# A decoder trunk step on one core: dense products inside the norm sums, the state copied by ScalarE, the next pair's first part beside the inverse, and steps that wait for a PSUM bank

## The chip, the cores and the metric

The kernel runs on one core of a Trainium2 chip. The time is device microseconds of one execution, the median of a few runs. The core has five engines that run their own instruction streams and wait for one another through semaphores: TensorE (PE in the profile, its weight loads PEld), VectorE (DVE), ScalarE (ACT), GpSimd (POOL) and SyncE (SP, which here only issues transfers).

## The reference, cut to what matters

One layer of a recurrent decoder trunk for 1024 prompt tokens and 8 sequences of 8 sample tokens (1088 columns, NT), width 1024, eight heads of 64. The recurrence of a head, whose matrix state is S:

```
def step(S, inp):
    r_t, w_t, k_t, v_t, kk_t, a_t = inp
    sa = einsum("bhvk,bhk->bhv", S, -kk_t)
    S = S * w_t + sa[..., None] * (kk_t * a_t) + v_t[..., None] * k_t
    y = einsum("bhvk,bhk->bhv", S, r_t)
    return S, y

h = adaLN(RMSNorm(x), c);  P = h @ w_in
r, k, v, xw, xa, xg = split(token_shift(P))
w_logit = w0 + tanh(xw) @ w2;  a = sigmoid(a0 + xa @ a2)
kk = k * k_k;  kk = kk * rsqrt(sum(kk * kk, per head) + 1e-12)
y = group_norm(scan(step)) + bonus;  o_r = y * (sigmoid(xg) @ g2)
merged = g_r * (o_r @ w_br_rwkv) + g_p * (o_p @ w_br_pool)
x = x + gate * (merged @ w_out)
x = x + gate2 * (relu(adaLN(RMSNorm(x), c) @ w_ff1) ** 2 @ w_ff2)
```

`o_p` comes from a pooling branch (running means over 2, 4, 8 and 16 tokens, then a small product per group).

## The kernel before

**Dense products.** An fp32 product is made of three products of rounded halves (`mm3`: high·high, high·low, low·high). A weight tile is split by ScalarE (`whi`, L193) and by VectorE or GpSimd (`wlo`, L194). A dense step is one 128x128 weight block on one of three column chunks (364, 362, 362): three TensorE products into an `mm` bank of PSUM. A job is a block of output rows: 72 such products with `w_in`. When a job is done, ScalarE mostly empties its banks (`px`, L531, L564, L582), and the next job opens three others. PSUM has eight banks: four `mm`, two `w` for the recurrence's steps, two `wc` for the state.

**First phase.** 34 jobs with `w_in`, then eight with `w_br` (`op_job`), run as a *back* stream. Between its steps runs *fore* work, generators that yield a time or a condition: `chains` (index 0), `heads` (1), `pools` (2), `or_rows` (3). TensorE's order is fixed by hand: `Pace.run` keeps a model clock `t`, which each product moves on by a modelled duration. A generator whose time has come takes the next turn, otherwise the back stream does. `Pace.warm` holds a step back until the last 3.4 us of the model hold enough dense work. The other engines' order is made by the framework from the order in which the program issues instructions.

**The recurrence** handles four pairs of heads, f = 0 to 3, in chunks of 64 tokens (two units u of eight chunks for the prompt, a third for the sample tokens):

- `front(f)`: squares of `kk`, `rinv` (the norm: nine products of a 128x128 block with the two columns `hsel`, two instructions each in TensorE's trace; root; reciprocal; spread over 64 columns on ScalarE), `spread` (128x128 transposes, `w<-kct,wt`), decay and gate logits (`w<-wt,sw`) with Tanh, then the cumulated decays `ev`, the scaled keys `bk` and the last decay of each chunk, `end`.
- `scores`: products of `ra` and `bk` for each unit, the bonus, transposes.
- `inverse` (a chain on VectorE), `level` (four steps of 32x32 products) and `affine`: `first` makes z·w and z·uv (`w<-at,z`, `w<-uv,z`), `second` (`w<-ab,at`) makes the transition matrix of each chunk in `ra[:, :, 1]`.
- `chain(f)`: sixteen state steps. Each is two products into `pn` (`wc<-ra,S`), the new S = S·end + pn on VectorE (L994), and two into `py`. Steps stand 2300 apart in the model's clock (1500 for the last pair).
- `sample(f)` and `post(f)`: the sample tokens' state, group norm (again `rinv` and `spread`) and gate. `post(3)` writes its result into the rows that the first job of phase 2 reads.

`heads` runs, for each f: `front(f)` and `scores(f)` side by side with `sample(f-1)`; then inverse, level and affine side by side with `post(f-1)`. `both` merges two generators: all of their steps that are due run within one turn of `Pace.run`. So `front(f+1)`, which needs nothing of the state, runs beside `chain(f)`.

**Second phase** (merge, output product, MLP, final norm) follows; its order is the same in both kernels.

Of the kernel before, what the change touches and what calls it, by code (L numbers as in the profile page):

```python
# [9 lines left out]
F32 = mybir.dt.float32  # L10
# [3 lines left out]
ALU = mybir.AluOpType  # L14
# [4 lines left out]
P = 128  # L19
# [60 lines left out]
class Pace:  # L80
# [3 lines left out]
    def __init__(self):  # L84
        self.t = 0.0
        self.work = []
        self.dense = False

# [15 lines left out]

    def run(self, back, fore=(), until=lambda: False):
        live = {i: 0.0 for i in range(len(fore))}
# [30 lines left out]
class K:  # L137
# [64 lines left out]
    def ps(self, tag):  # L202
        return (self.pc if tag == "wc" else self.pp).tile([P, 512], F32, tag=tag, bufs=PB[tag], name=self.nm(tag))
# [143 lines left out]
    def rinv(self, x, blocks, scale, eps, R):  # L347

        nc, k = self.nc, len(blocks)
        ps = self.ps("w")  # L350
        for i, b in enumerate(blocks):
            self.mm(ps[:, 2 * i:2 * i + 2], x[:, b:b + 128], self.kc("hsel"), start=True, stop=True)
        r = self.cp.tile([P, 9, 2], F32, tag="rh", bufs=3, name=self.nm("rh"))[:, :k, :]
        f = r.rearrange("p k h -> p (k h)")
        nc.scalar.activation(f, ps[:, :2 * k], AF.Sqrt, bias=self.eps[:, eps:eps + 1], scale=scale)
        nc.vector.reciprocal(f, f)
        i = 0
        for x in R:
            m = x.shape[1] // 128
            nc.scalar.activation(x.rearrange("p (k h j) -> p k h j", h=2, j=64), r[:, i:i + m, :].unsqueeze(3).to_broadcast([P, m, 2, 64]), AF.Copy)  # L360
            i += m
        return [x[:, o:o + 128] for x in R for o in range(0, x.shape[1], 128)]
# [286 lines left out]
    def front(self, f):  # L649
# [15 lines left out]
        yield self.pace.warm(8000 if f else 11000)  # L665
# [8 lines left out]
        for c0, n in FP:  # L674
            ps = self.ps("w")
            self.mm(ps[:, :n], w2a2[0:64, :], wa[0:64, c0:c0 + n], start=True, stop=True)
            nc.scalar.activation(t1[:, c0:c0 + n], ps[:, :n], AF.Tanh, bias=self.hp[:, f:f + 1], scale=0.5)
# [6 lines left out]
        nc.sync.dma_start(r, self.d_x[f])  # L684
        e = self.row(self.p1, "e", 1, w=1112)
# [6 lines left out]
        if f:  # L692
            yield lambda: ("c", f - 1, 0) in self.done
        for c0, n in FH:
            s, cs = slice(c0, c0 + n), slice(c0 // 64, (c0 + n) // 64)
            t, a, x = t1[:, s], tha[:, s], k[:, s]
            nc.vector.tensor_scalar(t, t, 1.0, None, op0=ALU.add)
            nc.vector.tensor_tensor_scan(t, self.kscan[:, s], t, 0.0, ALU.mult, ALU.add)  # L698
            m = min(n, NPR - c0)
# [9 lines left out]
            for h, hs in enumerate(HB):  # L709
                nc.vector.tensor_tensor(bk[hs, cs, h, :], cut(x[hs]), cut(t[hs]), op=ALU.mult)  # L710
                nc.vector.scalar_tensor_tensor(bk[hs, cs, 1 - h, :], cut(a[hs]), 0.5, cut(t[hs]), op0=ALU.mult, op1=ALU.mult)  # L711
            if c0 == 0:
                self.cur = dict(bk=bk, end=end, kk=kk, r=r, ev=ev, es=es, z=self.z, qs={})
                self.ra(self.cur, 0)
        nc.gpsimd.tensor_copy(end[:, 0:16], ev[:, :, 64])
        nc.gpsimd.tensor_copy(end[:, 16:24], es[:, :, 8])
# [5 lines left out]
        self.cur.update(q=q, v=v)  # L722

# [34 lines left out]
    def unit(self, f, d, u):  # L758
# [21 lines left out]
        yield 9000 if u == 0 else 3000 if u == 1 else 2000  # L780
# [150 lines left out]
    def affine(self, f, d):  # L931
# [4 lines left out]
        def first(u):  # L936
# [8 lines left out]
            nc.vector.tensor_copy(uv[HB[1], :, 0, :], cut(pu[HB[1], :]))  # L945
            nc.scalar.activation(uv[HB[0], :, 1, :], cut(pu[HB[0], :]), AF.Copy)

        def second(u):
            Q = d["qs"][u]
            ab, ra, w = Q["ab"], Q["ra"], Q["at"]  # L950
            pss = [self.ps("w") for _ in range(2)]
# [5 lines left out]
            for a, ps in enumerate(pss):  # L957
                pv = ps.rearrange("p (c s j) -> p c s j", s=2, j=64)
                us = slice(4 * a, 4 * a + 4)
                nc.scalar.activation(ra[:, us, 1, :], pv[:, :, 1, :], AF.Copy)  # L960
# [9 lines left out]
    def chain(self, f, d):  # L970

        nc = self.nc
        end = d["end"]
        S = None
        for u in range(2):
# [9 lines left out]
            for i in range(8):  # L985
                c = 8 * u + i
                at = slice(i * 64, (i + 1) * 64)
                S1 = self.sm.tile([P, 64], F32, tag="S", bufs=3, name=self.nm("S"))
                if S is None:
                    nc.vector.tensor_copy(S1, pn[:, at])  # L990
                else:
                    for hs in HB:
                        self.mm(pn[hs, at], ra[hs, i, 1, :], S[hs, :], start=False, stop=True, skip_group_check=True)
                    nc.vector.scalar_tensor_tensor(S1, S, end[:, c:c + 1], pn[:, at], op0=ALU.mult, op1=ALU.add)  # L994
# [148 lines left out]
    def heads(self):  # L1143

        for f in range(4):
            def lead():
                yield from self.front(f)
                yield from self.scores(f, self.cur)
# [8 lines left out]
            fill = self.post(f - 1) if f else self.ada_fill()  # L1157
            self.ds[f] = d

# [5 lines left out]
            yield from self.both(main(), fill)  # L1165
# [3 lines left out]
    def ada_fill(self):  # L1169
        wt = lambda: self.wt()[:, :1024]  # L1170
        asb = self.wt()[:, :512]
        yield from self.ada_part("w_ada_mix", 2, wt, asb, self.am, "b_mix", (16, 20), 5000)

# [17 lines left out]
    def chains(self):  # L1191
        for f in range(4):
# [53 lines left out]
    def phase1(self, ctx):  # L1246
# [38 lines left out]
        self.orr = [[None] * 4 for _ in range(2)]  # L1285
        self.pace.run(back, [self.chains(), self.heads(), self.pools(), self.or_rows()])
        nc.scalar.dma_start(io["o_ns"], self.ns)
# [764 lines left out]
```

## Time and profile before

| | us |
|---|---|
| median of three runs | 1656.93 |
| lowest and highest | 1653.72 and 1657.07 |
| the profiled execution, its own time | 1654.8 |
| its span in the trace | 1653.0 |
| TensorE busy in it | 1597.1 |
| VectorE, ScalarE, GpSimd busy | 1040.3, 721.7, 364.6 |

Rows of the profile name engine, line, operation and tiles as output<-inputs; `w<-ACT wt L677` among the waits says that a TensorE instruction that writes a `w` tile waited for ScalarE's instruction of line 677. The granted clock is the share of TensorE's full clock in a stretch (1.00 or 0.50 here). Line numbers are those of the kernel before; the kernel after has the dense product's line at 184 instead of 170 and the transpose's at 191 instead of 177.

### The profile page before, as it was taken

What the parts mean: (1) busy time and instruction counts of PE and PEld (TensorE: products, weight loads), DVE (VectorE), ACT (ScalarE), POOL (GpSimd) and SP (SyncE); (2) the same over time, 40 slices, a digit from 0 to 9 for tenths busy, and PEclk for the clock granted to TensorE, in tenths of its full rate; (3) what the DMA queues carried; (4) which work ended last, traced back from release to release, by engine and by line L of the source; (5) the groups of instructions that cost most, each with busy time, mean ns of one, the idle gap of its engine ahead of it and who ended that gap; (6) DMA issues with size and microseconds to landing.
All of it is one profiled execution on the core that took longest, in us unless ns stands there. A gap on an engine that the chain in (4) does not pass through costs nothing.

```text
span 1653.0 us, 35432 instructions
## 1 busy us (share of the span) xinstructions
PE 1597.1 (97%) x14331; PEld 1488.8 (90%) x14331; DVE 1040.3 (63%) x1800; ACT 721.7 (44%) x1414; POOL 364.6 (22%) x459
## 2 busy tenths in 40 slices
PE   6999999999999999999999999999999999999997
PEld 3989878887888889979989999999999999999997
DVE  5686547744675466334553696777555677877866
ACT  5543333343334333412233475545444765553323
POOL 3320101100000000001631332323233342521231
PEclk9999999999999999999999999999999999999999
DMA  9333413331332242375976455666665965675313
GB/s 338 111 110 135 139 48 119 117 102 67 113 109 92 80 136 102 103 295 174 348 251 227 131 181 180 220 226 240 232 222 204 347 202 190 195 247 182 99 39 109
DMA packets 123333, 279.43 MB, mean 169 GB/s; under 512 B 16769, under 2 KB 31105, under 8 KB 123169
## 3 DMA queue, kind: packets, MB, share of 16 engines
q1 hardware_dynamic: 107808, 228.52, 40.4%
q0 software_dynamic: 9312, 32.41, 5.9%
q10 hardware_dynamic: 6048, 16.23, 2.8%
q8 instruction: 113, 1.85, 0.5%
q14 instruction: 52, 0.42, 0.1%
HBM read 198.15 MB, written 78.95 MB: 168 GB/s over the span
## 4 chain that ended last, share of the span: by engine, by line
PE 82%; DVE 7%; ACT 4%; DMA 3%; issue 3%; POOL 1%; SPq 0%; DVEq 0%; ACTq 0%; POOLq 0%
PE mm L170 36%; PE pr L170 30%; PE w L170 11%; PE wc L170 4%; DMA wraw<-in_w_out 1%; PE w L177 1%; DVE hx L1729 1%; DMA x<-in_xT 1%; ACT whi L193 1%; DVE wlo L194 1%; DVE bk L711 0%; DVE wt L698 0%; POOL wlo L194 0%; DVE bk L710 0%; DMA wr<-in_w_ff 0%
## 5 line engine op out<-in xcount | busy, mean ns | idle before, releaser
L170 PE MATMUL mm<-hx,whi 128*128 128x362 f32 (+1 forms) x1920 | 507.8, 346 | 6.8 <-ACT px L564 2.9
L170 PEld LDWEIGHTS mm<-hx,whi 128*128 128x128 f32 x1920 | 334.0, 190 | 43.2 <-issue 18.5
L170 PE MATMUL pr<-mr,whi 128*128 128x272 f32 x1792 | 336.5, 287 | 0.6 <-DVE hx L1729 0.6
L170 PE MATMUL mm<-hx,wlo 128*128 128x362 f32 (+1 forms) x960 | 316.1, 329 | 0.0
L170 PEld LDWEIGHTS pr<-mr,whi 128*128 128x128 f32 x1792 | 280.7, 188 | 2.8 <-issue 2.8
L170 PE MATMUL pr<-mr,wlo 128*128 128x272 f32 x896 | 257.9, 288 | 0.2 <-DVE wlo L194 0.2
L193 ACT ACTIVATE whi<-wraw 128x512 fp32r<-128x512 f32 x186 | 116.9, 630 | 232.3 <-PE mm L170 68.9
L194 DVE TENSOR_TENSOR wlo<-wraw,whi 128x512 fp32r<-128x512 f32 x145 | 112.1, 773 | 121.1 <-ACT whi L193 120.9
L170 PEld LDWEIGHTS mm<-hx,wlo 128*128 128x128 f32 x960 | 182.9, 190 | 0.0
L170 PE MATMUL pr<-hx,whi 128*128 128x272 f32 x896 | 168.7, 287 | 1.4 <-DVE rs L1924 0.8
L170 PEld LDWEIGHTS pr<-mr,wlo 128*128 128x128 f32 x896 | 168.6, 188 | 0.4 <-DVE wlo L194 0.4
L170 PE MATMUL mm<-mr,whi 128*128 128x272 f32 (+4 forms) x736 | 152.3, 301 | 0.0
L170 PEld LDWEIGHTS pr<-hx,whi 128*128 128x128 f32 x896 | 140.3, 188 | 2.6 <-ACT whi L193 1.0
L193 ACT ACTIVATE whi<-wr 128x512 fp32r<-128x512 f32 x138 | 86.4, 628 | 112.6 <-PE pr L170 80.4
L170 PE MATMUL pr<-hx,wlo 128*128 128x272 f32 x448 | 128.9, 288 | 0.0
L170 PEld LDWEIGHTS mm<-mr,whi 128*128 128x128 f32 x736 | 119.2, 188 | 3.0 <-issue 2.5
L170 PE MATMUL mm<-mr,wlo 128*128 128x272 f32 (+4 forms) x368 | 110.2, 299 | 0.0
L194 POOL TENSOR_TENSOR wlo<-wraw,whi 128x512 fp32r<-128x512 f32 x41 | 55.3, 1349 | 245.8 <-ACT whi L193 245.6
L194 DVE TENSOR_TENSOR wlo<-wr,whi 128x512 fp32r<-128x512 f32 x103 | 77.2, 752 | 17.4 <-ACT whi L193 17.3
L170 PE MATMUL pr<-t,whi 128*128 128x272 f32 x448 | 84.6, 287 | 0.0
L170 PEld LDWEIGHTS pr<-hx,wlo 128*128 128x128 f32 x448 | 84.3, 188 | 0.0
L170 PEld LDWEIGHTS pr<-t,whi 128*128 128x128 f32 x448 | 70.2, 188 | 0.8 <-issue 0.8
(398 smaller groups left out, 2704.9 us busy)
## 6 DMA issues: line engine op xcount, KB each, us to landing
wr<-in_w_ff SPq DMA_DIRECT2D x137, 256.0 KB, 3.4
hid<-d_ch POOLq DMA_DIRECT2D x72, 272.0 KB, 3.7
wraw<-in_w_ff SPq DMA_DIRECT2D x71, 256.0 KB, 3.1
wraw<-in_w_in SPq DMA_DIRECT2D x68, 256.0 KB, 3.0
d_ch<-hx SPq DMA_DIRECT2D x52, 272.0 KB, 3.7
hid<-in_w_ada_mlp SPq DMA_DIRECT2D x24, 512.0 KB, 6.6
d_th<-px SPq DMA_DIRECT2D x22, 544.0 KB, 2.9
wt<-d_x SPq DMA_DIRECT2D x20, 544.0 KB, 4.3
```

What stands on the lines that cost most here:

```text
L170: return self.nc.tensor.matmul(out, lhsT, rhs, **kw)
L177: self.nc.tensor.transpose(out, in_, ident)
L193: nc.scalar.activation(hi, raw, AF.Copy)
L194: (nc.gpsimd if pool else nc.vector).tensor_tensor(lo, raw, hi.bitcast(F32), op=ALU.subtract)
L1729: nc.vector.tensor_tensor(acc, acc, v, op=ALU.add)
```

## The change

Four edits.

1. **Norm sums.** After every two products with `hsel`, `rinv` calls `pace.fill()`, which takes one dense step from the back stream. At its end ScalarE does a Tanh on one column, which loads Tanh's table again at that place.
2. **State.** `second` adds the diagonal matrix of the chunk's `end` to the transition matrix (GpSimd makes it, VectorE adds it while it empties the bank; before, ScalarE copied). The state step then is products and one ScalarE copy. The copies of `uv` and `end` go to ScalarE, too.
3. **Order of a pair.** `front` is cut in two. The first part, up to the Tanhs, runs for pair f + 1 beside inverse, level and affine of pair f, behind `post(f-1)`. The rest is `burst`, which gives way between its operations for f > 0 and stands beside `chain(f-1)`. Its wait for the state of the first unit moves to its end, ahead of `ra`. Some gaps change (Tanh steps 1300 to 2000; `warm` 8000 to 12000; the first unit's 9000 to 3000 for f > 0), and the first chain waits for the `w_ada_mix` part.
4. **Banks.** `Pace` models the two `w` banks. A step of `heads`, or a timed step of `pools`, is held back while both are taken. A step that opens banks takes them for 1500 to 3000 of the model's clock.

```diff
+    def fill(self):
+        if next(self.back, "idle") != "idle":
+            self.dense = True
     def run(self, back, fore=(), until=lambda: False):
...
                 r = live[i]
+                if self.taken is not None and i and self.banks[0] > self.t and (i == 1 or i == 2 and not callable(r) and self.t < r + 2500):
+                    continue
                 if r() if callable(r) else r <= self.t:
+                    if self.taken is not None:
+                        self.taken = 0
                     try:
                         r = next(fore[i])
+                        if self.taken:
+                            n = min(self.taken, 2)
+                            self.banks = sorted(self.banks[n:] + n * [self.t + (1500 if callable(r) else min(max(r, 1500), 3000))])
...
         for i, b in enumerate(blocks):
+            if i and i % 2 == 0:
+                self.pace.fill()
             self.mm(ps[:, 2 * i:2 * i + 2], x[:, b:b + 128], self.kc("hsel"), start=True, stop=True)
...
+        nc.scalar.activation(last, R[-1][:, 0:1], AF.Tanh)
...
-        yield self.pace.warm(8000 if f else 11000)
+        yield self.pace.warm(12000 if f else 11000)
...
-            yield 1300
+            yield 2000
...
-        if f:
-            yield lambda: ("c", f - 1, 0) in self.done
...
-        nc.gpsimd.tensor_copy(end[:, 0:16], ev[:, :, 64])
-        nc.gpsimd.tensor_copy(end[:, 16:24], es[:, :, 8])
+        nc.scalar.activation(end[:, 0:16], ev[:, :, 64], AF.Copy)
+        nc.scalar.activation(end[:, 16:24], es[:, :, 8], AF.Copy)
...
+        if f:
+            yield lambda: ("c", f - 1, 0) in self.done
+            self.ra(self.cur, 0)
...
-        yield 9000 if u == 0 else 3000 if u == 1 else 2000
+        yield (3000 if f else 9000) if u == 0 else 3000 if u == 1 else 2000
...
-            nc.vector.tensor_copy(uv[HB[1], :, 0, :], cut(pu[HB[1], :]))
+            nc.scalar.activation(uv[HB[1], :, 0, :], cut(pu[HB[1], :]), AF.Copy)
...
+            dg = cut(self.hv())
+            for hs in HB:
+                nc.gpsimd.tensor_tensor(dg[hs], self.kc("ident")[hs, hs].unsqueeze(1).to_broadcast([64, 8, 64]),
+                                        d["end"][hs, 8 * u:8 * u + 8].unsqueeze(2).to_broadcast([64, 8, 64]), op=ALU.mult)
...
-                nc.scalar.activation(ra[:, us, 1, :], pv[:, :, 1, :], AF.Copy)
+                nc.vector.tensor_tensor(ra[:, us, 1, :], pv[:, :, 1, :], dg[:, us, :], op=ALU.add)
...
-                    nc.vector.scalar_tensor_tensor(S1, S, end[:, c:c + 1], pn[:, at], op0=ALU.mult, op1=ALU.add)
+                nc.scalar.activation(S1, pn[:, at], AF.Copy)
...
-            fill = self.post(f - 1) if f else self.ada_fill()
+            def fill():
+                yield from self.post(f - 1) if f else self.ada_fill()
+                if f < 3:
+                    yield from self.front(f + 1)
```

How this moves TensorE's instructions, at three places. In these rows a name is output<-inputs, then the shape of the moving operand.

The norm sum of pair 1's front on TensorE before: nine products with `hsel` in one run, between a state step and dense products.

```order
L170 MATMUL wc_2496<-ra_1132,S_2720 64x64 x2
L170 MATMUL w_2753<-kct,wt_2667 128x2 x9
L170 MATMUL mm_2650<-hx_354,whi_2625 128x362
L170 MATMUL mm_2650<-hx_355,whi_2625 128x362
L170 MATMUL mm_2650<-hx_354,wlo_2626 128x362
```

The same norm sum in the changed kernel (its first three pieces), now earlier, behind the second affine step of pair 0.

```order
L184 MATMUL w_2483<-ab_1203,at_1206 64x128 x8
L184 MATMUL w_2504<-kct,wt_2320 128x2 x2
L184 MATMUL mm_2353<-hx_356,whi_2333 128x364
L184 MATMUL mm_2353<-hx_357,whi_2333 128x364
L184 MATMUL mm_2353<-hx_356,wlo_2334 128x364
L184 MATMUL w_2504<-kct,wt_2320 128x2 x2
L184 MATMUL mm_2354<-hx_356,whi_2333 128x362
L184 MATMUL mm_2354<-hx_357,whi_2333 128x362
L184 MATMUL mm_2354<-hx_356,wlo_2334 128x362
L184 MATMUL w_2504<-kct,wt_2320 128x2 x2
```

The run of nine has become pieces of two with three dense products between.

The logits of pair 1 (`w<-wt,sw`) on TensorE before, with a state product of the sample tokens (`x,z`) and the opening of a chain unit (`wc<-uv,ab`, `wc<-ab,uv`) behind them.

```order
L170 MATMUL w_2829<-wt_2671,sw_2664 128x512
L170 MATMUL w_2832<-wt_2671,sw_2664 128x512
L170 MATMUL w_2835<-x_2677,z 64x64 x2
L170 MATMUL wc_2840<-uv_1630,ab_1628 64x64 x16
L170 MATMUL wc_2841<-ab_1628,uv_1630 64x64 x16
L170 MATMUL wc_2840<-S_2781,ra_1625 64x64 x2
L170 MATMUL wc_2841<-ra_1625,S_2781 64x64 x2
L170 MATMUL w_2880<-wt_2671,sw_2664 128x288
L170 MATMUL w_2883<-wt_2671,sw_2664 128x288
```

In the changed kernel: the affine steps of pair 0's second unit, the opening of its chain (`wc`), and pair 1's transposes (L191); then, some rows on, the same logits.

```order
L184 MATMUL w_2546<-uv_1665,z 64x64
L191 MATMUL w_2582<-kct,wt_2320 128x128 x4
L184 MATMUL wc_2588<-uv_1205,ab_1203 64x64 x16
L184 MATMUL wc_2589<-ab_1203,uv_1205 64x64 x16
L184 MATMUL w_2627<-ab_1663,at_1666 64x128 x8
L184 MATMUL w_2628<-ab_1663,at_1666 64x128 x8
L191 MATMUL w_2649<-kct,wt_2320 128x128 x4
```

```order
L184 MATMUL w_2705<-wt_2324,sw_2317 128x512
L184 MATMUL w_2708<-wt_2324,sw_2317 128x512
L184 MATMUL wc_2588<-S_2655,ra_1179 64x64 x2
L184 MATMUL wc_2589<-ra_1179,S_2655 64x64 x2
L184 MATMUL mm_2690<-hx_348,whi_2466 128x364
L184 MATMUL mm_2690<-hx_349,whi_2466 128x364
L184 MATMUL mm_2690<-hx_348,wlo_2467 128x364
```

Six more dense products follow these before the next logits, so nine products stand between two uses of the `w` banks; in the affine string before them, transposes of one generator stand directly between the products of the other, with no dense product from the first affine product of this unit to the state step behind the last transpose.

The end of the recurrence on TensorE before: the last transposes (`w_8604`, `w_8610`) and the first rows behind them, which belong to jobs with `w_br`.

```order
L170 MATMUL mm_8557<-hx_8134,wlo_8489 128x364
L170 MATMUL mm_8558<-hx_8134,whi_8488 128x362
L170 MATMUL mm_8558<-hx_8136,whi_8488 128x362
L170 MATMUL mm_8558<-hx_8134,wlo_8489 128x362
L177 MATMUL w_8604<-kct,wt_8320 128x128 x4
L177 MATMUL w_8610<-kct,sw_8318 128x128
L170 MATMUL mm_8559<-hx_8134,whi_8488 128x362
```

The same place in the changed kernel; `mm_8801` is the first bank of phase 2's first job.

```order
L184 MATMUL mm_8687<-hx_8003,whi_8622 128x362
L184 MATMUL mm_8687<-hx_8005,whi_8622 128x362
L184 MATMUL mm_8687<-hx_8003,wlo_8623 128x362
L191 MATMUL w_8740<-kct,wt_8450 128x128 x4
L191 MATMUL w_8746<-kct,sw_8448 128x128
L184 MATMUL mm_8801<-hx_8007,whi_8775 128x364
```

Before, two whole jobs and three products (75) follow the last transposes inside the first phase; now none.

More of the change, by code (lines that the diff above doesn't have):

```diff
@@ L87, in __init__ @@
         self.dense = False
+        self.taken, self.banks = None, [0.0, 0.0]
     def spend(self, t, share):
@@ L202, in ps @@
     def ps(self, tag):
+        if tag == "w" and self.pace.taken is not None:
+            self.pace.taken += 1
         return (self.pc if tag == "wc" else self.pp).tile([P, 512], F32, tag=tag, bufs=PB[tag], name=self.nm(tag))
@@ L684, in front, with burst @@
         nc.sync.dma_start(r, self.d_x[f])
+        self.cur = dict(k=k, kk=kk, t1=t1, tha=tha, r=r)
+    def burst(self, f):
+        nc, io = self.nc, self.io
+        X = lambda b: lambda: ("X", b) in self.done
+        k, kk, t1, tha, r = (self.cur[x] for x in ("k", "kk", "t1", "tha", "r"))
+        step = lambda t: t if f else 0
         e = self.row(self.p1, "e", 1, w=1112)
@@ L698, in front @@
             nc.vector.tensor_tensor_scan(t, self.kscan[:, s], t, 0.0, ALU.mult, ALU.add)
+            yield step(1800)
             m = min(n, NPR - c0)
@@ L1143, in heads @@
     def heads(self):
+        yield from self.front(0)
         for f in range(4):
             def lead():
-                yield from self.front(f)
+                yield from self.burst(f)
                 yield from self.scores(f, self.cur)
@@ L1163, in main @@
                 yield from self.affine(f, d)
-            yield from self.both(main(), fill)
+            yield from self.both(main(), fill())
         yield from self.sample(3, d)
```

20 lines of the change are left out of this document (13 added, 7 removed).

## The prediction

> **What bounds the kernel now.** I read the page first, then the table by stage, then TensorE's waits, then its clock, then its timeline.
>
> ```profile
> PE 1597.1 (97%) x14331; PEld 1488.8 (90%) x14331; DVE 1040.3 (63%) x1800; ACT 721.7 (44%) x1414; POOL 364.6 (22%) x459
> 0.00:50.00 50.00, 34.94 (x177) 20.30 (x178) 31.98 (x57) 25.35 (x37) 18.23 (x39) 0.97 0.89 296
> 50.00:850.00 800.00, 774.70 (x8043) 694.14 (x8042) 460.27 (x856) 297.41 (x634) 102.35 (x158) 0.99 0.39 135
> 850.00:1653.00 803.00, 787.47 (x6116) 774.39 (x6114) 548.05 (x888) 398.93 (x744) 244.05 (x263) 1.00 0.57 195
> ```
>
> The columns of the last three rows are: stretch, length, busy time (and instructions) of PE, PEld, DVE, ACT, POOL, then the granted clock, DMA share and GB/s. TensorE is the bound, 97% busy. The change touches only the stage from about 50 to 850 us, where the recurrence runs between dense products; start and second phase keep their order. In that stage TensorE is idle for 800.00 − 774.70 = 25.3 us. The change neither adds nor removes a product, so it can gain only those 25.3 us, and what a lowered clock costs. TensorE's waits in the stage, longest first (engine, destination, line, what ended the wait; total us, times, longest):
>
> ```profile
> PE w L170 <- ACT wt L677: 5.7, 8, 2.0
> PE wc L170 <- DVE S L994: 4.3, 4, 2.8
> PE mm L170 <- ACT px L564: 2.9, 3, 1.8
> PE w L170 <- DVE wt L1115: 1.9, 2, 1.0
> PE mm L170 <- ACT px L582: 1.5, 1, 1.5
> PE w L170 <- issue: 1.3, 1, 1.3
> PE mm L170 <- DVE px L1319: 1.2, 1, 1.2
> PE w L170 <- DVE px L642: 1.2, 3, 0.6
> ...
> PE w L177 <- ACT z L928: 0.7, 1, 0.7
> PE w L177 <- ACT wt L360: 0.7, 1, 0.7
> PE w L170 <- ACT at L944: 0.7, 1, 0.7
> ```
>
> The rows into `w` add to 5.7 + 1.9 + 1.2 + 0.7 + 0.7 + 0.7 = 10.9 us (1.3 more has no releaser): a head step opens one of two `w` banks before ScalarE or VectorE has emptied it. The rows into `mm` (2.9 + 1.5 + 1.2 = 5.6 us) are dense products waiting for an evacuation. 4.3 us are waits for the state S.
>
> The granted clock is 0.99, not 1. Stretches around the places where it falls (same columns):
>
> ```profile
> 230.37:233.78 3.41, 3.41 (x33) 3.22 (x32) 2.46 (x6) 1.90 (x4) 0.00 (x0) 1.00 0.10 32
> 233.79:237.20 3.41, 3.41 (x19) 2.89 (x18) 0.28 (x1) 1.63 (x4) 0.00 (x0) 0.50 0.12 43
> 421.52:424.93 3.41, 0.65 (x4) 0.34 (x3) 3.35 (x8) 0.00 (x0) 0.03 (x1) 1.00 0.22 72
> 424.94:428.34 3.40, 3.38 (x17) 3.26 (x18) 2.02 (x3) 0.47 (x1) 0.00 (x0) 0.50 0.72 211
> 561.47:564.87 3.40, 3.40 (x15) 3.40 (x15) 0.27 (x1) 1.62 (x4) 0.00 (x0) 0.50 0.00 0
> 564.88:568.29 3.41, 3.41 (x18) 2.81 (x18) 0.28 (x1) 0.38 (x1) 0.00 (x0) 0.50 0.03 10
> ```
>
> There are six such half-clock stretches in the stage: these four, and 401.04 to 404.45 and 517.10 to 520.50. Two follow idle time (421.52: busy 0.65 of 3.41 us, waiting for S). Four follow or contain a norm sum, with TensorE 'busy' throughout: 18 products of two columns each. TensorE's timeline there:
>
> ```profile
> 229.91 0.49 PE L170 MATMUL mm<-hx,whi 128*128 128x364 f32 x2
> 230.24 0.33 PE L170 MATMUL mm<-hx,wlo 128*128 128x364 f32 x1
> 230.50 0.33 PE L170 MATMUL wc<-S,ra 64*64 64x64 f32 x4
> ...
> 230.88 2.17 PE L170 MATMUL w<-kct,wt 128*128 128x2 f32 x18
> ...
> 234.14 0.81 PE L170 MATMUL mm<-hx,whi 128*128 128x364 f32 x2
> 234.75 0.50 PE L170 MATMUL mm<-hx,wlo 128*128 128x364 f32 x1
> ...
> 244.78 0.33 PE L170 MATMUL w<-x,z 64*64 64x64 f32 x4 [2.05 <-ACT wt L677]
> ```
>
> Two dense products start 0.33 us apart at 229.91, 0.165 each; at 234.14 0.61, 0.305 each. A half-clock stretch of dense products thus loses 3.41 × (1 − 0.165 / 0.305) = 1.6 us, six at most 9.4; since small products beside them lose less I count 8.
>
> **The change part by part.** *Norm sums.* The 18 narrow products took 2.17 us, about 0.11 each, and keep that; between every two now stands one dense step of three products (0.5 us). Same work, other order; a split costs between nothing and the longer first dense product (at 229.91 a pair takes 0.49; behind such a run I see up to 0.09 more), so 31 splits cost 0 to 2.8 us. I take 1, with the few further changes of tile shape. In return any 3.4 us then hold more dense work than narrow: I expect three of the four stretches behind norm sums to go, and one of the two behind idle time, since its wait goes: 4 × 1.35 = −5.5 us (bounds 0 and −8).
>
> [...]
>
> *Bank waits.* The model of the pace now holds a head step back while both `w` banks are taken, and tanh steps wait 2000 instead of 1300. The 2.05 us at 244.78 is such a place: two 512-wide and two state products stood directly behind one another; now nine dense products (1.5 us) stand between. But steps merged side by side (inverse and the next front) run back to back without that check: the four SPREAD products now stand directly behind the 32 of the first affine step, whose banks are emptied by ScalarE copies of 0.6 us. I added up, for each reuse of a bank in the new order, the products that cover it, at the durations above: about 9 us remain of 12.2 (10.9 + 1.3). I take −3; bounds −10 and +3.
>
> *State.* Rows that carry this (line, engine, operation, shapes, count | busy us, mean ns | idle before):
>
> ```profile
> L994 DVE SCALAR_TENSOR_TENSOR S<-S,end,wc 128x64 f32<-128x64 f32 x60 | 16.7, 278 | 31.4 <-PE wc L170 25.6 <-PE w L170 5.1
> L533 ACT ACTIVATE px<-mm 128x64 f32<-128x64 f32 x13 | 3.0, 228 | 0.0
> L960 ACT ACTIVATE ra<-w 128x256 f32<-128x256 f32 x16 | 5.9, 380 | 10.8 <-PE w L170 10.8
> L961 DVE TENSOR_TENSOR ra<-ra,w 128x256 f32<-128x256 f32 x16 | 6.6, 420 | 15.0 <-ACT ra L960 14.7
> L946 ACT ACTIVATE uv<-w 64x512 f32<-64x512 f32 x8 | 4.7, 591 | 3.1 <-DVE uv L945 3.1
> L355 ACT ACT_TABLE_LOAD x8 | 10.3, 1283 | 0.1
> L194 POOL TENSOR_TENSOR wlo<-wraw,whi 128x512 fp32r<-128x512 f32 x14 | 18.6, 1326 | 144.7 <-ACT whi L193 144.7
> ```
>
> 60 state updates of 278 ns leave VectorE; 64 copies of about 228 ns come to ScalarE. The 16 copies of L960 (380) become 16 additions of 420 on VectorE; eight uv copies (0.59) move to ScalarE; the table loads rise by 4 net (1.28). ScalarE: 64 × 0.228 + 8 × 0.59 + 4 × 1.28 − 16 × 0.38 = +18.4 us on 297 of 800: cover is ample, TensorE's dense stream hides it. VectorE: 16 × 0.42 − 60 × 0.278 = −10, and eight uv copies less. POOL gets 16 diagonal blocks of 64x512, each dearer than nothing and cheaper than L194's 1.33, at most 21 on 102; at their place 15 dense products (2.5 us) stand before the product that needs them. On the path only the waits for S count: 4.3 us in four, when a state update stood behind a burst of 0.75 us operations on VectorE. Those go, and the burst is cut into pieces; on ScalarE S stands behind at most a weight split or three copies. I take −2.3 (bounds −4.3 and +15, the last in the rivals).
>
> [...]
>
> *Dense banks.* Tanh's table comes back right behind the norm sum's copies, no longer at the next evacuation that needs it (L564), so I take −1.5 of the 5.6 us (bounds −4 and +4), and −1 for what else of the 25.3 is left.
>
> *End of the stage.* Before, 75 dense products follow the last SPREAD before the first product on the last pair's rows can be due; now those rows' job starts directly behind it, and only its first 27 products need nothing of them: 27 × 0.165 = 4.5 us. In that time VectorE and ScalarE must finish the last pair. The rows, of the earlier pairs and of the job that ends there:
>
> ```profile
> L1115 DVE SCALAR_TENSOR_TENSOR wt<-wt,part,w 128x512 f32<-128x512 f32 x8 | 5.9, 744 | 8.3 <-PE w L177 8.3
> L1117 DVE SCALAR_TENSOR_TENSOR wt<-wt,part,wt 128x576 f32<-128x576 f32 x4 | 4.3, 1066 | 0.1
> L1118 DVE TENSOR_TENSOR wt<-wt,wt 128x576 f32<-128x576 f32 x4 | 3.0, 758 | 0.1
> L1137 ACT ACTIVATE wt<-wt 128x1088 fp32r<-128x1088 f32 x3 | 3.3, 1113 | 8.4 <-DVE wt L1118 8.4
> L1138 DVE TENSOR_TENSOR wt<-wt,wt 128x1088 fp32r<-128x1088 f32 x3 | 3.9, 1292 | 3.9 <-ACT wt L1137 3.9
> ```
>
> 0.74 + 0.28 (the 64-wide one, as S) + 1.07 + 0.76, then half of L1137 and of L1138 (0.56 + 0.65) make 4.1 us, and up to three updates of the finished job (some 0.5 each) stand ahead: 4.1 to 5.6 against 4.5. I take +1 (0 to 3).
>
> **Sum:** −5.5 + 1 − 3 − 2.3 − 1.5 − 1 + 1 = −11.3 us. Against the profiled execution's span of 1653.0 that is 1641.7. The median of the runs (1656.93) lies 3.9 above that span, the profiled run's own time (1654.8) 1.8; against the median I forecast 1656.9 − 11.3 = **1646**, with an own range of 1638 to 1652.
>
> **Rivals.** *(a) Nearly everything goes.* All six half-clock stretches (−8) and two thirds of the 25.3 us idle (−17): 1632. For it: bank waits and S waits have one place each that the edits name. Against it: about 9 us of bank reuse is still short of cover.
>
> *(b) The clock stays and the banks only shift.* Narrow products among dense ones may still count as a quiet stretch, or the new string of 64-column products of affine, chain and SPREAD without a dense one between becomes quiet in its turn; against the second, the string from 244.78 on is of that kind and kept full clock. Clock 0, banks 0, the other terms stand: 1 − 2.3 − 1.5 − 1 + 1 = −2.8; 1654. [...]
>
> *(c) Slower: ScalarE's queue stands behind S.* Before, VectorE waited 25.6 us for S's products (60 updates, 0.43 each) and nothing of the dense stream stood behind it. Now ScalarE waits in order, and it empties the `mm` banks. A job needs three of four banks, so at each job's end the second chunk of the next one waits for an evacuation with some 1 us to spare. If an evacuation stands behind an S copy whose product comes a step later (2.3 us in the pace's clock), 1.3 us are lost; some three job ends fall in each pair's chain, 12 in all: +15.6, and two further clock stretches, +3.2. With the forecast's −11.3 that makes +7.5: 1664. The point from which it decides is 11.3 / 12 = 0.9 us per job end. For it: `mm` already waits 5.6 us on evacuations. Against it: the average wait is 0.43, inside the slack.
>
> **How the numbers follow.** Forecast 0.52, (a) 0.13, (b) 0.18, (c) 0.17. The range runs from 1632, (a)'s middle, to 1661, short of (c)'s: outside lie half of (a), 0.06, and most of (c), 0.13. What can't be told from no change is ±0.2%, 3.3 us: 1653.6 to 1660.2. Faster: 0.50 of the forecast, all of (a), 0.07 of (b), 0.70. Same: the forecast's last 0.02, 0.10 of (b), 0.01 of (c), 0.13. Slower: the rest, 0.17.
>
> **What would show it.** In the changed profile: idle time of TensorE from 50 to 850 near 17 instead of 25 us; waits on S gone from VectorE and under 2 us on ScalarE; at most three half-clock stretches in the stage, none behind a norm sum; the rows into `w` near 9 us, now with the affine step's copies among the releasers; a gap of about 1 us in the last product job of the first phase. Wrong it is if a half-clock stretch still follows the split norm sums, if `mm` waits grow by more than 4 us, or if the stage is shorter but the second phase longer.

## The result, and the profile after

The changed kernel takes **1647.87 us** (median of seven runs, 1645.08 to 1653.89) against 1656.93 of the kernel before (seven runs). The ratio is 0.9943 with a 95% interval of 0.9921 to 0.9964: 9 us faster. Repeated later with more runs it is 1649.37 against 1657.78, ratio 0.9949 (0.9931 to 0.9968).

The profile after is of the slowest of the seven runs: 1653.89 us, span 1652.1. A comparison of the two spans (1653.0 and 1652.1) would hide the change. The page's first part, and the windows of the stage up to the first product of the second phase, which begins at 783.8 us before and at 777.2 after (columns as in the prediction). First the kernel after:

```profile
PE 1598.5 (97%) x14331; PEld 1492.5 (90%) x14331; DVE 1019.8 (62%) x1744; ACT 738.9 (45%) x1491; POOL 365.9 (22%) x467
```

```profile
50.00:777.00 727.00, 706.59 (x7606) 630.57 (x7605) 406.99 (x742) 293.13 (x676) 66.97 (x131) 0.98 0.35 121
777.00:1652.00 875.00, 857.50 (x6555) 842.25 (x6553) 581.38 (x947) 421.02 (x781) 280.67 (x297) 0.99 0.58 202
```

The same two stretches of the kernel before:

```profile
50.00:784.00 734.00, 708.70 (x7607) 629.71 (x7606) 423.66 (x803) 277.73 (x602) 63.90 (x123) 0.99 0.35 120
784.00:1653.00 869.00, 853.47 (x6551) 838.82 (x6549) 584.66 (x943) 418.61 (x777) 282.50 (x297) 1.00 0.59 203
```

The stage became 7 us shorter: idle time 25.3 → 20.4 us, busy time 2.1 less. The second phase, whose order is the same, took 6 us more in this execution (4.6 more in the second profile below), with two half-clock stretches from 862.3 us that the profile before does not have. Of the later profiles, that of the split alone (at 863.0) and that of the state copy alone (at 860.0), both in the old order, have such a stretch there too, so it is not shown to come from the change. TensorE's waits in the stage after:

```profile
PE w L184 <- DVE px L632: 4.8, 1, 4.8
PE w L184 <- ACT iv L833: 4.0, 4, 1.6
PE w L191 <- ACT at L977: 2.6, 4, 0.7
PE w L184 <- issue: 2.2, 2, 1.9
PE w L191 <- ACT uv L979: 1.7, 3, 0.6
...
PE w L184 <- ACT at L977: 1.7, 1, 1.7
...
PE w L184 <- ACT uv L857: 1.1, 2, 0.5
PE wc L184 <- ACT S L1027: 0.8, 1, 0.8
PE mm L184 <- ACT px L551: 0.6, 1, 0.6
```

Waits for S fell from 4.3 to 0.8 us, those of `mm` from 6.1 (all rows that name a releaser) to 0.6. The rows into `w` rose from 13.2 to 18.7, "issue" counted (a row of 0.8 before, behind TensorE itself, is left out). Two of the waits are new and do not concern a bank: the first product of a pooling group comes before VectorE has finished its running sums, whose last operation is line 632 (at 315 us the wait stands as "issue", but line 632 ends at 314.99 and the product starts at 315.09). Together they are 6.7 us, against 1.3 at such a place before. What is left, 12.0, is what it was (11.9). Windows around 509 us show the price of such a wait: 0.56 us busy, then half clock.

```profile
503.91:507.32 3.41, 0.56 (x4) 0.26 (x2) 3.41 (x7) 0.63 (x1) 2.52 (x5) 1.00 0.00 0
507.33:510.70 3.37, 1.44 (x3) 0.90 (x4) 1.75 (x6) 0.44 (x1) 0.32 (x1) 0.50 0.26 78
```

**Half-clock time.** Each run has its span and mean granted clock. In the profiles before and after the clock is 1 or 0.5 in every stretch, so (1 − clock) × 2 × span is taken as the time spent at half clock. Its mean is 35.9 us before (34 runs) and 30.8 after (18 runs); in the two first profiles 6 to 8 us of it lie at the very end of the span and 3.4 ahead of 50 us, where the change does nothing. One us of it costs an estimated 1 − 0.165 / 0.305 = 0.46 us of dense products, from the two starts of dense products in the profile before (229.91 and 234.14 us); across the 105 runs of all experiments the span rises by 0.36 us for each, within a kernel. It differs by some 7 us (one standard deviation) from run to run of the same kernel, and it accounts for some six tenths of the variance of their spans.

The traces before and after show one thing more. The half-clock stretches in them stand on a grid with steps of some 3.41 us: those of the profile before, from 233.79, 401.04, 424.94, 517.10 and 561.47 us on, lie 49, 7, 27 and 13 such steps apart; those of the profile after, from 80.66, 114.81, 316.18, 381.04, 507.33 and 862.32 us on, 10, 59, 19, 37 and 104. The wait for the tile `asb` early in the second phase lies differently on it in the two. In the profile before, it is 2.46 us, ends at 866.1, and falls on two steps, both at full clock (the first two rows). In the profile after, it is 2.91 us, ends at 863.1, and most of it falls on one step, with half clock behind it (the last two). The wait is longer, too (2.91 against 2.46 us); whether its place or its length matters was not tested.

```profile
861.86:865.26 3.40, 1.80 (x15) 1.59 (x13) 1.66 (x3) 0.96 (x2) 0.00 (x0) 1.00 0.64 186
865.27:868.67 3.40, 2.54 (x21) 2.54 (x22) 0.92 (x2) 1.40 (x3) 1.26 (x1) 1.00 0.99 354
858.90:862.31 3.41, 1.27 (x10) 1.05 (x9) 1.75 (x3) 1.05 (x2) 0.07 (x1) 1.00 0.59 185
862.32:865.70 3.38, 2.62 (x12) 2.62 (x13) 0.99 (x2) 1.33 (x3) 1.27 (x1) 0.50 1.01 365
```

### The profile page after: what moved, and what is told of

It is laid out like the page before. It is cut to its first block, busy times and chain, and to the rows that moved or that the text cites. A ratio compares the mean times of both kernels' runs of the same rounds, so it can differ in the third digit from the quotient of the medians.

```text
span 1652.1 us, 35483 instructions
## 1 busy us (share of the span) xinstructions
PE 1598.5 (97%) x14331; PEld 1492.5 (90%) x14331; DVE 1019.8 (62%) x1744; ACT 738.9 (45%) x1491; POOL 365.9 (22%) x467
## 4 chain that ended last, share of the span: by engine, by line
PE 61%; ACT 2%; DVE 2%; DMA 2%; issue 1%; POOL 1%; SPq 0%; DVEq 0%; POOLq 0%; ACTq 0%
PE pr L184 32%; PE mm L184 21%; PE w L184 6%; PE wc L184 2%; DMA wraw<-in_w_out 1%; DVE hx L1772 0%; DMA wt<-d_x 0%; POOL t L1410 0%; PE w L191 0%; ACT whi L207 0%; DVE hx L1941 0%; POOL wr L1745 0%; ACT mr L1695 0%; ACT hx L1695 0%; DMA wraw<-in_w_ff 0%
```

## The experiments

Ratios are to the kernel before on the same chip; idle is TensorE's from 50 us to the first product of the second phase, in the one profile; half-clock time is the mean over the runs.

| run | median us | ratio, 95% interval | half clock us | idle us |
|---|---|---|---|---|
| before | 1655.6 to 1657.8 | | 35.9 | 25.3 |
| changed, again | 1649.37 | 0.9949 (0.9931 to 0.9968) | 32.1 | 21.7 |
| changed, norm sums in one run | 1656.14 | 0.9991 (0.9975 to 1.0008) | 43.6 | 21.6 |
| changed, state on VectorE | 1658.01 | 1.0006 (0.9991 to 1.0021) | 43.3 | 23.3 |
| changed, no bank model | 1655.58 | 0.9978 (0.9961 to 0.9994) | 32.2 | 26.3 |
| changed, old order of the pairs | 1668.99 | 1.0066 (1.0047 to 1.0085) | 50.0 | 29.6 |
| changed, squares later | 1651.88 | 0.9969 (0.9951 to 0.9986) | 32.4 | 20.3 |
| changed, pooling jobs later | 1656.55 | 0.9990 (0.9977 to 1.0003) | 33.4 | 24.7 |
| before, split norm sums alone | 1649.88 | 0.9953 (0.9934 to 0.9972) | 25.9 | 21.1 |
| before, state copy alone | 1647.75 | 0.9942 (0.9924 to 0.9961) | 26.4 | 19.7 |
| changed, squares on GpSimd | 1645.60 | 0.9935 (0.9915 to 0.9955) | 29.1 | 19.4 |
| the same, wider gap in the first unit | 1644.54 | 0.9913 (0.9894 to 0.9933) | 25.2 | 19.7 |
| before, split and state part | 1644.32 | 0.9925 (0.9897 to 0.9952) | 23.5 | 17.2 |

### The changed kernel again

> The changed kernel itself, so that what follows is compared on the same chip, and for a second profile: the first one (span 1652.1 us) is of the slowest of seven executions. Theory 1, an unlucky execution: a span of 1643 to 1648 us, at most five half-clock stretches between 50 and 850 us where the first profile has seven, and one or none in the second phase where it has two; the waits of TensorE stay as they are, among them 4.8 us for line 632. Theory 2, the waits make the clock fall each time: again seven stretches in the stage and a span near 1651.

Neither theory held whole. The span of the profiled run was 1650.8 us with six half-clock stretches in the stage and one in the second phase; the waits were the same, 4.8 us for line 632 among them. Over eleven runs the span lay between 1644.8 and 1654.2. So the long waits came again (4.8 us behind line 632 and 4.0 behind line 833 in both profiles), while the half-clock stretches went from seven and two to six and one.

### The dense products all ahead of the norm sum

```diff
+        for _ in range((k - 1) // 2):
+            self.pace.fill()
         for i, b in enumerate(blocks):
-            if i and i % 2 == 0:
-                self.pace.fill()
             self.mm(ps[:, 2 * i:2 * i + 2], x[:, b:b + 128], self.kc("hsel"), start=True, stop=True)
```

> The same dense products are taken from the back stream, but all ahead of each norm sum, whose narrow products again stand in one run; the rest of TensorE's order stays. Theory 1 (the prediction: a run of narrow products makes the clock fall): two to four half-clock stretches behind norm sums come back, +2 to +6 us against the changed kernel. Theory 2 (only idle time makes it fall, or the split costs as much as it brings): within 1 us of the changed kernel, stretches only behind idle time.

6.8 us slower than the changed kernel, with the same idle time (21.6 against 21.7) and 43.6 instead of 30.8 us at half clock: 12.8 × 0.36 to 0.46 is 4.6 to 5.9 us. That is theory 1, a little above its range. Its one profile has seven stretches in the stage, no more than the first profile after, but three of them (524.2, 558.4 and 684.7 us) stand behind norm sums. Its windows around one norm sum, and TensorE's timeline there:

```profile
554.98:558.39 3.41, 3.41 (x34) 3.33 (x33) 0.94 (x2) 2.42 (x4) 0.00 (x0) 1.00 0.15 31
558.40:561.80 3.40, 3.40 (x13) 3.33 (x12) 0.01 (x1) 2.83 (x5) 0.00 (x0) 0.50 0.14 49
```

```profile
555.73 2.06 PE L184 MATMUL w<-kct,wt 128*128 128x2 f32 x18
557.73 0.33 PE L184 MATMUL wc<-S,ra 64*64 64x64 f32 x4
557.89 0.28 PE L184 MATMUL wc<-ra,S 64*64 64x64 f32 x4
558.11 0.77 PE L184 MATMUL mm<-hx,whi 128*128 128x362 f32 x2
```

TensorE is busy for 3.41 of 3.41 us and yet the next stretch is at half clock: 2.06 us of the time go to 18 products of two columns. By busy time alone this is not to be seen.

### The state back on VectorE

```diff
...
-                nc.vector.tensor_tensor(ra[:, us, 1, :], pv[:, :, 1, :], dg[:, us, :], op=ALU.add)
+                nc.scalar.activation(ra[:, us, 1, :], pv[:, :, 1, :], AF.Copy)
...
-                nc.scalar.activation(S1, pn[:, at], AF.Copy)
+                if S is None:
+                    nc.scalar.activation(S1, pn[:, at], AF.Copy)
+                else:
+                    c = 8 * u + i
+                    nc.vector.scalar_tensor_tensor(S1, S, d["end"][:, c:c + 1], pn[:, at], op0=ALU.mult, op1=ALU.add)
```

The diagonal on GpSimd goes with it.

> Only the state's copy is undone: VectorE again computes S times end plus the product, ScalarE again copies the transition matrix; order of TensorE unchanged. Theory 1 (the prediction): waits for S on VectorE come back, 2 to 4 us, and the time rises by 2 to 4 us. Theory 2 (cutting the burst in pieces was enough): waits for S under 1 us, time within 1 us. Theory 3 (ScalarE's queue behind S hurts the dense banks): faster than the changed kernel by over 1 us.

The mechanism of theory 1, at twice its size: 8.6 us slower. TensorE's waits of this run have this row:

```profile
PE wc L184 <- DVE S L1027: 3.8, 4, 2.7
```

So 3 us of waits came back (idle time as a whole rose by 1.6 to 2.9 against the two profiles of the changed kernel), and with them 43.3 − 30.8 = 12.5 us at half clock, another 4.5 to 5.8 us. Together that is 6 to 9 us. Cutting the burst in pieces did not do it, and theory 3 is excluded.

### Without the model of the banks

```diff
-        self.pace.taken = 0
         self.pace.run(back, [self.chains(), self.heads(), self.pools(), self.or_rows()])
```

> The model of the two w banks is left out, so steps are no longer held back; the rest of the change stays, the order of TensorE shifts in many places. Theory 1 (the prediction): idle time of TensorE from 50 to 850 us rises by 3 to 8 us, all of it in rows into w, and the time by 3 to 8 us. Theory 2 (the waits only change place): idle time and time within 2 us of the changed kernel.

Theory 1 in size: idle time 26.3 against 20.4 and 21.7, 6.2 us slower, half-clock time nearly the same. Most of the new waits are into `w`, above all behind line 833, which empties such a bank and took 4.0 us in the changed kernel; some 2 us are into `mm`:

```profile
PE w L184 <- ACT iv L833: 8.6, 6, 1.6
```

### The old order of the pairs

```diff
-        yield from self.front(0)
         for f in range(4):
             def lead():
+                yield from self.front(f)
                 yield from self.burst(f)
...
-                if f < 3:
-                    yield from self.front(f + 1)
```

with the gaps, the place of the wait for the first unit and the missing wait for `w_ada_mix` of the kernel before.

> Only the move of the next pair's first part is undone: front and burst run in one piece beside the chain, with the gaps of the kernel before; split norm sums, state copy and bank model stay. The three parts undone so far each cost 6 to 9 us (1656.1, 1658.0 and 1655.6 against 1649.4), together more than the whole gain of 8.4 us. Theory 1, the new order is a loss that the others pay for (stalls on line 632 and line 977 come with it): 1 to 10 us faster than the changed kernel, and these two waits gone. Theory 2, the order gains too, and each part undone costs more than it brings alone, since every new stall also lowers the clock: 3 to 9 us slower, with the waits for S on ScalarE behind the burst.

The direction of theory 2, but far beyond its size: by the medians 19.6 us slower than the changed kernel and 12.5 slower than before. Its mechanism is not what the trace shows: the named wait for S was 1.6 us only. The largest row of its waits, its longest wait, and the end of its stage on TensorE:

```profile
PE w L184 <- issue: 10.1, 5, 6.5
```

```profile
515.10 1.55 PE L184 MATMUL w<-px,plw 128*128 128x364 f32 x2 [6.48 <-issue]
...
793.01 1.17 PE L184 MATMUL w<-kct,wt 128*128 128x2 f32 x10
796.27 0.66 PE L191 MATMUL w<-kct,wt 128*128 128x128 f32 x4 [2.09 <-ACT wt L379]
```

The longest wait, 6.5 us, is again the first product of a pooling group: VectorE's line 632 ends at 514.98 us. And the last norm sum has no dense product left to stand between, as the recurrence's steps were held back until they reached the end of the dense stream. The last run below, which differs from this one in the bank model alone, shows that the model costs that much in this order; its own wait for line 632 is 1.6 us.

### Squares later, and squares on GpSimd

In the changed kernel the copy that empties a bank (line 977) stands on ScalarE behind the squares of the next pair, which wait for their transfer. ScalarE's timeline after:

```profile
378.34 1.39 ACT L680 ACTIVATE wt<-wt,part 128x512 f32<-128x512 f32 x2 [4.24 <-DMA wt<-d_x]
379.63 0.57 ACT L977 ACTIVATE at<-w 128x512 f32<-128x512 f32 x1
```

```diff
         nc.sync.dma_start(k, self.d_x[4 + f])
+        if f:
+            yield 6000
...
-        yield self.pace.warm(12000 if f else 11000)
+        yield self.pace.warm(6000 if f else 11000)
```

> The changed kernel with the squares of the next pair's keys issued 6 us (of the pace's clock) behind the transfer that they read, with TensorE's order kept. In the changed kernel a square waits in ScalarE's queue 4.2 us for that transfer, and the copy that empties a w bank (line 977) stands behind it: TensorE waits 1.7 to 2.0 us at 380 us and a half-clock stretch follows in all three profiles with this order. Theory 1 (ScalarE's queue): that wait and that stretch go, -2 to -4 us. Theory 2 (the bank would be late anyway): wait and time within 1 us.

The wait (1.7 us) and the order on ScalarE stayed, so this run tells nothing of the theories: the framework sorts ScalarE's instructions, and it put the squares ahead of the copy again. The second attempt takes them off ScalarE:

```diff
-            nc.scalar.activation(kk[:, c0:c0 + n], k[:, c0:c0 + n], AF.Square, scale=self.par("k_k", f))
+            if f:
+                nc.gpsimd.tensor_scalar(kk[:, c0:c0 + n], k[:, c0:c0 + n], self.par("k_k", f), None, op0=ALU.mult)
+                nc.gpsimd.tensor_tensor(kk[:, c0:c0 + n], kk[:, c0:c0 + n], kk[:, c0:c0 + n], op=ALU.mult)
+            else:
+                nc.scalar.activation(kk[:, c0:c0 + n], k[:, c0:c0 + n], AF.Square, scale=self.par("k_k", f))
```

> The changed kernel with the squares of pairs 1 to 3 on GpSimd instead of ScalarE, so that no square waits for its transfer ahead of the copy of line 977; in the run with the later squares the framework had put them ahead of it all the same. Theory 1 (ScalarE's queue): TensorE's wait of 1.7 us at 380 and the half-clock stretch that tends to follow go, -1 to -4 us. Theory 2 (the bank would be late anyway): wait and time within 1 us.

The wait of 1.7 us is gone, so ScalarE's queue was its cause. In its place the norm sum waits for the squares on GpSimd:

```profile
PE w L184 <- POOL wt L682: 1.0, 1, 1.0
```

The median is 4 us below the changed kernel's, but the intervals overlap; the profile alone gives 0.7 us, and whether there is more is open.

### Pooling jobs later

```diff
-            jobs += [Q[g], G[2 * g], G[2 * g + 1]]
+            jobs += [G[2 * g], Q[g], G[2 * g + 1]] if g % 2 else [Q[g], G[2 * g], G[2 * g + 1]]
```

> The changed kernel with the second and fourth pooling job each one dense job later, so that VectorE's running sums no longer fall into the inverse of a pair. Theory 1 (line 632 is late because the sums stand between the inverse's transposes on VectorE): the waits of 4.8 us at 509 and 1.9 us at 315 go, with two or three half-clock stretches behind them, -6 to -11 us. Theory 2 (the product of the pooling group is placed too early whatever VectorE does): the wait moves with the job, time within 2 us.

A miss, 7 us slower. The wait of 4.8 us at 509 went, but VectorE's part of the pooling then fell among the affine steps. Rows of its waits:

```profile
PE w L184 <- issue: 5.1, 3, 2.6
...
PE w L184 <- DVE px L662: 3.1, 3, 1.8
PE wc L184 <- ACT S L1027: 2.8, 2, 2.0
...
PE w L191 <- DVE px L662: 2.2, 1, 2.2
```

The wait at 315, which belongs to the first group, was untouched (1.9 us): I had ascribed it to the wrong job.

### A wider gap in the first unit, beside the squares on GpSimd

```diff
-            yield 2800
+            yield 4500 if u == 0 and f == 0 and a == 0 else 2800
```

> As the run before it, and the two halves of the first pair's first unit stand 4500 instead of 2800 apart in the pace's clock. In the changed kernel the second half waits 0.6 and 1.5 us at 113 and 115 for ScalarE's copies of line 833 that stand behind a 1.3 us operation on VectorE, and two half-clock stretches follow in every profile. Theory 1: these waits and stretches go, 3 to 6 us faster than the changed kernel in all. Theory 2 (the later steps of the recurrence are pushed past the end of the dense stream): no faster than the run before it, with a longer wait at the end of the stage.

The waits at 113 and 115 shrank to one of 0.7, but idle time is as before (19.7 against 19.4): the later steps shifted, and line 977 now costs 4.4 us and S 2.4. The median is 4.8 us below the changed kernel's, inside theory 1's range, and the half-clock stretches behind 113 us are gone from the profile. But behind the wait for S, which ends at 713.5, half clock lasts for 13.6 us with TensorE busy throughout, so the profile (the slowest of its six runs) does not show a gain. The ratio, 0.9913, is the best of all, but its interval overlaps the neighbours'; a gain over the run before it is not shown.

### The split alone, the state copy alone, and both, in the old order

The edits are those of the change, put into the kernel before: `fill` in `rinv`; the diagonal and the copy of S; then both, with the copies of `uv` and `end` and Tanh's reload, but without bank model and moved front.

> The kernel before with the split norm sums alone. Undone in the changed kernel they cost 6.7 us, all of it as half-clock time. Theory 1 (the split is worth its clock stretches wherever it stands, as the prediction's 5.5 us less 1): 3 to 6 us faster than before, half-clock time per run down by 8 to 14 us from 36. Theory 2 (non-additive: in the old order the idle places lower the clock anyhow): within 2 us of before.

> The kernel before with the state's copy on ScalarE and the diagonal in the transition matrix alone; TensorE's order is the old one. Undone in the changed kernel this part cost 8.6 us. Theory 1 (the wait for S goes from VectorE's queue, as the prediction's 2.3 us): waits for S from 4.3 to under 2 us, 1 to 5 us faster than before. Theory 2 (worth the same 8.6 us here): 6 to 10 us faster. Theory 3 (the prediction's slower rival, ScalarE's queue behind S): waits of mm on ScalarE's evacuations grow from 4.9 us by more than 3, slower than before.

> Split norm sums and the whole of the state part (copies of S, uv and end on ScalarE, diagonal, Tanh's reload) in the order of the kernel before, without the bank model and without the moved front. Alone the split gave a ratio of 0.9953 to before, the state copy 0.9942; both with the bank model in the old order gave 1.0066. Theory 1 (the two parts add, and the bank model is what made that run slow by pushing the recurrence past the dense stream): 0.987 to 0.992, some 1637 to 1645 us, faster than the whole change. Theory 2 (the parts don't add, since a stall removed at one place only moves the wait): 0.993 to 0.998. Theory 3 (the old order itself is bad once S is on ScalarE behind the burst and Tanh's loads): at or above 1.

Each alone brings about as much as the whole change: the split 7.8 us, the state copy 9.9. For the split theory 1 holds in direction, but 7.8 us is above its 3 to 6, and only half of it is the clock: half-clock time fell by some 10 us, worth 3.6 to 4.6, and idle time in the one profile by 4.2. For the state copy no row with S is left among the waits, and `mm` waits less, too, so theory 3 is excluded here as well; the size is that of theory 2. Two rows of its waits, the first the same as before:

```profile
PE w L170 <- ACT wt L677: 5.7, 8, 2.0
...
PE mm L170 <- ACT px L564: 0.9, 2, 0.4
```

Its time adds up: idle 25.3 → 19.7 and half-clock time 35.9 → 26.4, together 5.6 + 9.5 × 0.36 to 0.46 = 9.0 to 10.0.

Both together give 0.9925, 11.3 us, between the ranges of theories 1 and 2; theory 3 is excluded. The sum of the two (0.9895) lies just outside the interval but has an error of its own, and the interval also overlaps that of each part alone, so how far they add stays open. It is no slower than the whole change, whose interval it overlaps. With the bank model added in this order the run above gave 1.0066, that is 1.4% more: idle 17.2 → 29.6 and half-clock time 23.5 → 50.0, 12.4 + 26.5 × 0.46 = 24.6 us. With the moved front added and no bank model it gave 0.9978, again slower, and the intervals don't touch. So, with split and state copy in place, the front's move costs, the bank model in the old order costs more, and only both together come out even. Neither was run alone on the kernel before.

## Why the prediction held, and where it did not

The forecast was 1646 with a range of 1632 to 1661. The median, 1647.87, is 9.1 us below before where 11.3 were forecast. That the sum came so close is in part luck. Of the forecast, 4.5 us were clock (with the price of the splits) and 6.8 idle time. Measured, the clock brings 1.8 to 2.3 us (5.1 us of half clock at 0.36 to 0.46) and idle time 4.9 in the first profile, 3.6 in the second: 5.4 to 7.2 of the 8.4 to 9.1 us. The rest is not accounted for. Among the terms some errors cancel, and two of the three signs that I had named for being wrong did appear: a half-clock stretch behind a split norm sum, and a shorter stage with a longer second phase (though the runs do not show the latter to come from the change). Idle time from 50 to 850 us is 22.0, not near 17.

- **Norm sums, −5.5.** The mechanism is shown: with idle time unchanged, putting the narrow products back in one run costs 6.8 us, 4.6 to 5.9 of them as half-clock time, and the split alone saves 7.8, half of it as half-clock time. Inside the change the clock's net gain is smaller: 35.9 → 30.8 us at half clock, some 2 us, and new half-clock stretches stand at new idle places (from 507.33 us on at the wait of 4.8 us, from 381.04 on behind that of 1.7). I predicted at most three half-clock stretches in the stage, none behind a norm sum; there were seven and six, one of them from 80.7 us on inside a split norm sum that also held 0.64 us of idle time.
- **Splits, +1.** No cost shows: the split alone has 4.2 us less idle time than before and the time falls by more than that.
- **Bank waits, −3.** This step failed. "About 9 us remain of 12.2": counted with the small rows that the prediction leaves out it was 13.2, and it is 18.7: 12.0 beside the pooling groups, where it was 11.9, and 6.7 at the pooling groups, where it was 1.3. I had added up the products that cover each bank reuse, but the new waits are for VectorE's data and ScalarE's queue, which that count leaves out. The model is still worth its place in the new order: without it the kernel is 6.2 us slower. That steps merged in `both` bypass the check is seen as foretold (the transposes, L191, behind lines 977 and 979: seven waits, 4.3 us in all).
- **State, −2.3.** The wait that I named went (4.3 → 0.8), so the mechanism was right. The term was mis-sized, since it counted the waits for S only, and one half-clock stretch beside them under the norm sums: alone the copy is worth 9.9 us, 5.6 of idle time and the rest at half clock.
- **Dense banks, −1.5.** `mm` fell by 5.5 us, also mis-sized. Which part did it was not isolated; the state copy alone already brings line 564 from 2.9 to 0.9.
- **End of the stage, +1.** No gap: VectorE's chain ended 4.8 us after the stage, and TensorE's timeline has no wait there up to 786 us. The term is 0, the lower bound.

Rival (b), that the clock stays, is excluded as a mechanism by the run with the norm sums in one piece, though its "banks only shift" is what happened. Rival (c), ScalarE's queue behind S, is excluded: S waits 0.8 and `mm` 0.6 us. Its kind of stall did occur with another instruction, the squares at 378. The clock fell at the gap of 4.8 us at 509 (half clock from 507.33 on), behind gaps of 1.7 us (381.04, after) and 2.8 us (424.94, before) too, and with no gap at all: TensorE was busy for 3.41 of 3.41 us ahead of 233.79 in the profile before, and ahead of 558.40 in the run with the norm sums in one piece.

One slip of bookkeeping: I took the median as 3.9 above the span. Every run's time is 1.8 above its own span; the other 2 us were the execution that happened to be profiled.

## What to carry to other kernels

Count a stall at two prices: its own length and the time at half clock that came with it. Here the state copy alone saved 5.6 us of idle time and 9.5 us at half clock, an estimated 3.4 to 4.4 us; undone in the changed kernel it brought 1.6 to 2.9 us of idle time and 12.5 at half clock, an estimated 4.5 to 5.8 us. Look for runs of narrow products too, which the busy share does not show (3.41 of 3.41 us ahead of the half clock at 558.40). When a change has several parts, run each alone: here two small ones carry the whole gain, and a large reordering with a scheduler's rule to support it came out even. A count of cover for one resource is no forecast of waits as long as the queues of the other engines are not in it: here it gave 9 us into `w`, and 18.7 were measured.

## What the runs showed of the hardware

Half-clock time differed between executions of the changed kernel by 7.4 us (standard deviation of 18 runs), though its longest waits were the same (4.8 and 4.0 us in both profiles). So here it takes several profiles, or the clock of many runs, to judge a term of this kind.

Runs of 18 two-column products did not always lower the clock. With the state copy alone, where every norm sum is one run, the profile has two half-clock stretches in the stage, back to back from 511.8 us. They follow the norm sum at 508.89, with a wait of 2.98 us ahead of it; the other six norm sums of nine blocks have none behind them. In the kernel before, three of the seven have one. What decides at which of them the clock falls stays open.

```profile
508.30:511.70 3.40, 3.09 (x24) 2.81 (x23) 0.54 (x1) 3.35 (x5) 0.00 (x0) 1.00 0.00 0
511.80:515.20 3.40, 3.40 (x69) 2.59 (x68) 0.86 (x2) 2.86 (x8) 0.64 (x1) 0.50 0.00 0
```
